# A hybrid decoder block: the first half's output projection with two of its four pairs of rows as seven-product units, and the mixers' outputs stored whole

## The chip, the cores and the metric

One core of a Trainium2 chip runs the whole layer in one launch. The metric is the device time of one execution in microseconds (us); lower is better. The engines are PE (matmuls; its weight loads are shown as PEld), DVE, ACT and POOL (elementwise work), and SP, which in this kernel issues every DMA, in the order of its own list. Each engine works through its list strictly in order.

## The reference

The layer takes x (2048 positions, 1024 columns, float32) through two mixers and an FFN:

```python
h = rmsnorm(x, norm1_g);  proj = h @ w_in
# mixer A: gated linear attention (GLA), 4 heads, chunks, a running state
o = rmsnorm(gla_chunked(q, k, v, log_a), gla_norm_g) * silu(p_g)      # 512 columns
# mixer B: gated short convolution
o_conv = c_b * causal_depthwise_conv(c_c * c_h, conv_w)               # 512 columns
x = x + concat([o_gla, o_conv]) @ w_out                               # 1024 x 1024
h2 = rmsnorm(x, norm2_g)
x = x + (silu(h2 @ w_ffn_gate) * (h2 @ w_ffn_up)) @ w_ffn_down        # 2816 wide
return rmsnorm(x, norm_f_g)
```

The line with `w_out` is the output projection that the change is about.

## The kernel before, in words

**Layout.** Everything is kept transposed: a tile has 128 columns of the model as partitions and 512 positions as elements. The 2048 positions are four blocks, two to a half; `half` and `j` count them. The 1024 columns are 8 tiles of 128. The output projection of a half therefore makes 8 rows of tiles, two blocks wide, each a sum over 8 tiles `k` of the mixers' outputs (k = 0 to 3 from GLA, 4 to 7 from the convolution).

**Float32 from pieces.** An operand is split in a high part (`split`, L162: ACT rounds it) and a low part (DVE subtracts). A product of two split tiles is three matmuls of 128x128 by 128x512: high-high, high-low, low-high. Weights are split on the way as well (`weight_quarter`, L404).

**Seven products.** Most of the kernel's products are 2x2 blocks: two rows of tiles by two blocks of positions, over operands halved in k. `unit` (L452) makes the four result blocks from seven products rather than eight, by sums and differences of the weights' quarters (A11, A12, A21, A22 and S1 to S4, `unit_weights`, L424, four POOL operations and seven splits) and of the operands (B11, B12, B21, B22 and T1 = B12 - B11, T2 = B22 - T1, T3 = B22 - B12, T4 = B21 - T2). A product is one block sum of `len(op)` slices of three matmuls (`product_step`, L443). The result blocks are put together by DVE additions (L473); with `onto` each product is added onto a given tile in SBUF as soon as it is there, and the third product goes on in the PSUM bank of the first.

**The output projection before** (`out_proj`, L935) doesn't use units: it takes the rows in four pairs (`d0` = 0, 2, 4, 6), and for each pair runs over k, with four PSUM banks, 12 matmuls for each k. In the middle of a pair it loads the residual's tiles y (from `xt`, L956); at the end DVE adds the banks to them (L970), SP stores them to `sx`, and ACT and POOL add up their squares (L921) for the next norm. Its weights come from `plain_weights` (L912): one load of 1 MB and four splits for a pair.

**The mixers' outputs before** are split where they are made and stored as pairs of high and low parts: the convolution's at L794 to L798, the GLA's at L907 to L909. `build_mix` (L929) loads pairs of 512 KB, with nothing left to do on ACT and DVE.

**What sets the order.** The body (L1250 on) runs the input projection of both halves, then `out_proj(0)`, `out_proj(1)`, then the FFN. Between matmul groups `tick` (L241) takes a step of background generators; the GLA of the second half runs so beside the first half's output projection. While the second output projection runs, `h2_first` and `h2_rest` make the FFN's first operands. A scheduler that works on the whole program then fixes each engine's list. Buffers come from pools with a fixed number of slots: 28 operand slots (`opp`, each for a high and a low part), 9 tiles `tp` (y, squares, results), 4 split weights `wqp`, 2 raw weights, 8 PSUM banks. A load into a slot stands in SP's list and waits there until the slot's last reader is done; everything behind it in the list waits too. The input unit before `out_proj(0)` fills all 28 operand slots; the plain projection needs 16.

Of the kernel before, what the change touches and what calls it, by code (L numbers as in the profile page):

```python
# [10 lines left out]
F32 = mybir.dt.float32  # L11
# [41 lines left out]
def tile_hymba_block(ctx, tc, x, xt, win, wa, wgu, wout, wffn, wdown, wdown_first, small, out):  # L53
# [57 lines left out]
    s_mix = [[dram.tile([P, 2, PB], F32, name=f"sm{b}_{k}") for k in range(4)] for b in range(NB)]  # L111
    s_gla = [dram.tile([P, HEADS, 2, PB], F32, name=f"sgla{b}") for b in range(NB)]
# [291 lines left out]
    def weight_quarter(src):  # L404

        n = src.shape[-1]
# [7 lines left out]
        split(src, h[:, 0, :], h[:, 1, :])  # L414
        return h
# [8 lines left out]
    def unit_weights(src, raw=None):  # L424
        raw = raw_weights(src) if raw is None else raw
        n = src.shape[-1]
        a11, a12, a22, a21 = [raw[:, i, :] for i in range(4)]
        s1 = rawp.tile([P, PB], F32, name="s1", tag="s1", bufs=1)[:, 0:n]
        w = {"A11": weight_quarter(a11)}
        pool.tensor_tensor(s1, a21, a22, ALU.add)  # L430
# [10 lines left out]
        return w  # L441

    def product_step(o, w, op, k, first):  # L443
# [3 lines left out]
        xh, xl = op[k][:, 0, :], op[k][:, 1, :]  # L447
# [301 lines left out]
    def in_proj(half, ops, first=None, differences=None):  # L749
# [22 lines left out]
        for i0 in (0, 2):  # L772
# [128 lines left out]
    def gla_finish(b, t, osb, g):  # L901
# [26 lines left out]

    def build_mix(half):  # L929
# [5 lines left out]
    def out_proj(half, ops, ahead=None, rest=None):  # L935
        ssq = []
        ws = chain.from_iterable(plain_weights(wout[u], 4) for u in range(4))
        for d0 in range(0, KD, 2):
            o = {(e, j): bank() for e in range(2) for j in range(2)}
            for k in range(KD):  # L940
                for e in range(2):
                    wh, wl = next(ws)
                    for j in range(2):
                        m = ops[k][j]
                        pe.matmul(o[e, j][:], wh, m[:, 0, :], start=k == 0, stop=False)  # L945
                        pe.matmul(o[e, j][:], wh, m[:, 1, :], start=False, stop=False)  # L946
                    for j in range(2):
                        pe.matmul(  # L948
                            o[e, j][:], wl, ops[k][j][:, 0, :], start=False, stop=k == KD - 1
                        )  # L950
# [318 lines left out]
    ssq = out_proj(0, build_mix(0))  # L1269
# [118 lines left out]
```

## Time and profile before

| what | value |
|---|---|
| median of 3 runs | 2060.9 us (2059.68 to 2062.77) |
| span of the profiled execution | 2059.3 us |
| busy share PE, DVE, ACT, POOL | 98%, 69%, 47%, 42% |
| first half's output projection, first matmul | at 569.6 us |
| second half's output projection, last matmuls | at 759 us |

Of the profiled execution the span is the one time that is given. Lines of a trace read: start, duration, engine, line of the kernel, operation, tile written <- tiles read, count, and in brackets the idle time ahead of it with what ended it. Group lines read: line, engine, operation, tiles, shape and count, then busy time, mean ns of one, and the idle time before. Lines of DMA issues read: tiles, queue, count, KB each, median us from issue to landing.

### The profile page before, as it was taken

The numbers are of one execution on the slowest core, as the hardware profiler recorded it, in microseconds if no ns is written. First come the engines' busy times: TensorE is split into PE (matmuls) and PEld (weight loads), VectorE is DVE, ScalarE is ACT, GpSimd is POOL, SyncE is SP. The second block draws the span as 40 slices with busy tenths as digits, with TensorE's granted clock in tenths as the row PEclk, the third lists the DMA queues.
The fourth block names the chain that finished last, engine by engine and source line by source line (L and its number), as shares of the span: only waits on it lengthen the run. The fifth ranks groups of instructions, "written<-read, shape, count | busy, mean of one in ns | idle before, by whom it ended". The sixth has DMA issues, their size and how long they took to land.

```text
span 2059.3 us, 27063 instructions
## 1 busy us (share of the span) xinstructions
PE 2018.4 (98%) x9229; PEld 1657.3 (80%) x9229; DVE 1425.3 (69%) x2128; ACT 959.7 (47%) x1918; POOL 859.8 (42%) x622
## 2 busy tenths in 40 slices
PE   7999999999999999999999999999999999999997
PEld 6877888787888888888888878787888888878786
DVE  8789686559743886676675676767666666667774
ACT  6655365765542344444444452334434444453344
POOL 0345322122102564464564345534644544435544
PEclk9999999999999999999999999999999999999998
DMA  6378485416586873545454676476444434586653
GB/s 229 116 274 278 159 319 165 143 67 194 190 296 246 311 254 130 198 181 207 156 185 143 241 264 254 185 282 257 163 164 167 175 140 169 179 309 223 234 217 126
DMA packets 188729, 421.47 MB, mean 205 GB/s; under 512 B 19792, under 2 KB 65072, under 8 KB 178992
## 3 DMA queue, kind: packets, MB, share of 16 engines
q1 hardware_dynamic: 188592, 419.76, 57.2%
q8 instruction: 72, 1.18, 0.2%
q14 instruction: 65, 0.53, 0.1%
HBM read 274.98 MB, written 144.70 MB: 204 GB/s over the span
## 4 chain that ended last, share of the span: by engine, by line
PE 84%; DVE 7%; DMA 4%; ACT 3%; issue 1%; POOL 1%; SPq 0%; DVEq 0%; ACTq 0%; POOLq 0%
PE mm L448 24%; PE mm L449 23%; PE mm L450 23%; PE mm L945 3%; PE mm L948 3%; PE mm L946 3%; DVE wq L164 2%; DVE op L164 1%; DMA op<-sa_B 1%; DMA op<-sa_T 1%; PE a_ps L702 1%; ACT wq L163 1%; DMA siT<-lo 1%; PE o_ps L869 1%; PE o_ps L871 1%
## 5 line engine op out<-in xcount | busy, mean ns | idle before, releaser
L448 PE MATMUL mm<-op,wq 128*128 128x512 f32 x2499 | 973.7, 392 | 10.3 <-ACT c L480 5.3
L449 PE MATMUL mm<-op,wq 128*128 128x512 f32 x2499 | 972.5, 390 | 1.6 <-DVE op L164 1.6
L450 PE MATMUL mm<-op,wq 128*128 128x512 f32 x2499 | 961.3, 390 | 2.6 <-DVE wq L164 2.3
L164 DVE TENSOR_TENSOR wq<-raw,wq 128x512 fp32r<-128x512 f32 (+2 forms) x626 | 508.9, 818 | 262.6 <-ACT wq L163 260.0
L163 ACT ACTIVATE wq<-raw 128x512 fp32r<-128x512 f32 (+2 forms) x626 | 364.9, 589 | 585.6 <-PE mm L450 447.9
L448 PEld LDWEIGHTS mm<-op,wq 128*128 128x128 f32 x2499 | 468.9, 188 | 114.9 <-ACT c L480 8.0
L450 PEld LDWEIGHTS mm<-op,wq 128*128 128x128 f32 x2499 | 469.1, 188 | 103.8 <-DVE wq L164 6.1
L449 PEld LDWEIGHTS mm<-op,wq 128*128 128x128 f32 x2499 | 469.3, 188 | 99.1 <-DVE op L164 3.7
L432 POOL TENSOR_TENSOR raw<-s,raw 128x512 f32<-128x512 f32 (+2 forms) x97 | 133.3, 1374 | 518.5 <-DVE wq L164 474.7
L430 POOL TENSOR_TENSOR s<-raw 128x512 f32<-128x512 f32 (+2 forms) x97 | 127.4, 1313 | 247.5 <-DMA raw<-in_wffn_dram 90.7
L473 DVE TENSOR_TENSOR c<-mm,c 128x512 f32<-128x512 f32 x198 | 135.8, 686 | 72.7 <-PE mm L450 70.9
L473 DVE TENSOR_TENSOR y<-mm,y 128x512 f32<-128x512 f32 x185 | 126.9, 687 | 83.3 <-PE mm L450 82.9
L437 POOL TENSOR_TENSOR raw<-raw 128x512 f32<-128x512 f32 (+2 forms) x97 | 120.6, 1244 | 126.7 <-DVE wq L164 126.7
L927 POOL TENSOR_TENSOR ssx<-ssx,q 128x512 f32<-128x512 f32 x52 | 77.4, 1504 | 158.8 <-ACT q L926 158.5
L431 POOL TENSOR_TENSOR raw<-raw 128x512 f32<-128x512 f32 (+2 forms) x97 | 137.3, 1416 | 4.9
L480 ACT ACTIVATE c<-mm 128x512 f32<-128x512 f32 x198 | 116.1, 587 | 11.1 <-PE mm L450 9.3
L945 PE MATMUL mm<-op,wq 128*128 128x512 f32 x256 | 100.9, 395 | 0.0
L946 PE MATMUL mm<-op,wq 128*128 128x512 f32 x256 | 99.7, 389 | 0.0
L163 ACT ACTIVATE wq<-s 128x512 fp32r<-128x512 f32 (+2 forms) x97 | 56.9, 587 | 89.3 <-PE mm L450 85.4
L164 DVE TENSOR_TENSOR wq<-s,wq 128x512 fp32r<-128x512 f32 (+2 forms) x97 | 82.6, 852 | 2.8 <-ACT wq L163 2.1
L164 DVE TENSOR_TENSOR op<-op 128x512 fp32r<-128x512 f32 x94 | 76.8, 844 | 4.7 <-ACT op L163 4.6
L948 PE MATMUL mm<-op,wq 128*128 128x512 f32 x256 | 79.8, 390 | 0.0
(204 smaller groups left out, 1807.6 us busy)
## 6 DMA issues: line engine op xcount, KB each, us to landing
raw<-in_wffn_dram SPq DMA_DIRECT2D x44, 1024.0 KB, 6.5
sa_B<-so SPq DMA_DIRECT2D x47, 512.0 KB, 4.2
op<-sa_B SPq DMA_DIRECT2D x47, 512.0 KB, 7.1
raw<-in_win_dram SPq DMA_DIRECT2D x23, 1024.0 KB, 5.4
sa_T<-so SPq DMA_DIRECT2D x44, 512.0 KB, 4.5
op<-sa_T SPq DMA_DIRECT2D x44, 512.0 KB, 6.9
raw<-in_wdown_dram SPq DMA_DIRECT2D x24, 768.0 KB, 5.8
sx<-y SPq DMA_DIRECT2D x48, 256.0 KB, 4.0
```

The lines of the kernel that those rows point to most:

```text
L163: last_hi[:] = [act.activation(hi, src, AF.Copy)]
L164: last_lo[:] = [dve.tensor_tensor(lo, src, hi.bitcast(F32), ALU.subtract)]
L430: pool.tensor_tensor(s1, a21, a22, ALU.add)
L431: pool.tensor_tensor(a21, a11, a21, ALU.subtract)
L432: pool.tensor_tensor(a11, s1, a11, ALU.subtract)
L448: pe.matmul(o[:], wh, xh, start=first and k == 0, stop=False, skip_group_check=True)
L449: pe.matmul(o[:], wh, xl, start=False, stop=False, skip_group_check=True)
L450: return pe.matmul(o[:], wl, xh, start=False, stop=k == n - 1, skip_group_check=True)
L473: dve.tensor_tensor(t[:], o[:], t[:], ALU.add)
L945: pe.matmul(o[e, j][:], wh, m[:, 0, :], start=k == 0, stop=False)
L946: pe.matmul(o[e, j][:], wh, m[:, 1, :], start=False, stop=False)
L948: pe.matmul(o[e, j][:], wl, ops[k][j][:, 0, :], start=False, stop=k == KD - 1)
```

## The change

The mixers' outputs are stored whole, as float32 (half the bytes, no split at the mixers), and split when they are loaded for the output projection, in both halves (`load_whole`).

The second half's projection is otherwise as before. In the first half's, the pairs d0 = 0 and 2 stay plain; d0 = 4 and 6 become two units of seven products, with 4 slices each (84 matmuls a unit) and `onto` the residual. `build_mix_sevens` lays the operands of both forms into the 28 slots: a slot holds the whole value in one half and the high part in the other, and for all but B21 a second slot holds the low part. While the plain pairs run, a generator `making` takes 16 steps, one for each k of the two pairs. For each of four slices POOL makes T1, T3, T2 and T4 (16 operations); T1, T2 and T3 are split over the whole values that are no longer needed. T4 is stored to DRAM and, in the second pair from its fifth k on, loaded and split over B12's high and low part (`fourth`), which only the plain pairs read.

In the units, the loads of the residual y stand at the start of each unit; each product is added onto y; the finished rows are stored and their squares added up after the unit. The weights of a unit are taken from the same 1 MB as those of a plain pair, read with a stride.

```diff
-    s_mix = [[dram.tile([P, 2, PB], F32, name=f"sm{b}_{k}") for k in range(4)] for b in range(NB)]
-    s_gla = [dram.tile([P, HEADS, 2, PB], F32, name=f"sgla{b}") for b in range(NB)]
+    s_mix = scratch("sm", 4)
+    s_gla = [dram.tile([P, HEADS, PB], F32, name=f"sgla{b}") for b in range(NB)]
+    s_mix4 = [dram.tile([P, PB], F32, name=f"smt{k}") for k in range(4)]
...
                 dve.tensor_tensor(y[:], c[:], y[:], ALU.mult)
-                hi = tp.tile([P, PB], F32R, name="hi", tag="t")
-                split(y[:], hi[:], y[:].bitcast(F32R))
-                dst = s_mix[2 * half + j][i0 + r]
-                store(dst[:, 0, :], hi[:].bitcast(F32))
-                store(dst[:, 1, :], y[:])
+                store(s_mix[2 * half + j][i0 + r][:], y[:])
...
         dve.scalar_tensor_tensor(osb[:], ot[:], col(C_GN), g[:], ALU.mult, ALU.mult)
-        split(osb[:], g[:].bitcast(F32R), osb[:].bitcast(F32R))
-        for e, y in enumerate((g, osb)):
-            store(s_gla[b][:, :, e, t * P : (t + 1) * P], y[:])
+        store(s_gla[b][:, :, t * P : (t + 1) * P], osb[:])
...
     def build_mix(half):
-        def pair(b, k):
-            return load_pair(s_gla[b][:, k] if k < HEADS else s_mix[b][k - HEADS])
-
-        return [[pair(2 * half + j, k) for j in range(2)] for k in range(KD)]
+        return [[load_whole(mixed(2 * half + j, k)) for j in range(2)] for k in range(KD)]
+
+    def build_mix_sevens():
...
+        for k in range(KD):
+            row = []
+            for j in range(2):
+                n = "B" + str(1 + k // 4) + str(1 + j)
+                o = b[n, k % 4] = slot()
+                load(whole(o), mixed(j, k))
+                lo = o[:, 1, :]
+                if n != "B21":
+                    x = t[n, k % 4] = slot()
+                    lo = x[:, 0, :]
+                split(whole(o), o[:, 0, :], lo)
...
+        def divide(y, n, m, k):
+            x = b[m, k][:, 1, :], t[m, k][:, 1, :]
+            split(y[:], *x)
+            sevens[n].append(x)
+
+        def making():
+            for k in range(4):
+                b11, b12, b22 = [whole(b[n, k]) for n in ("B11", "B12", "B22")]
+                y, z, b21 = [tt(n) for n in ("ty", "tz", "b21")]
+                load(b21[:], mixed(0, k + 4))
+                pool.tensor_tensor(y[:], b12, b11, ALU.subtract)
+                pool.tensor_tensor(z[:], b22, b12, ALU.subtract)
+                yield
+                divide(y, "T1", "B11", k)
+                divide(z, "T3", "B12", k)
+                yield
+                pool.tensor_tensor(y[:], b22, y[:], ALU.subtract)
+                yield
+                divide(y, "T2", "B22", k)
+                pool.tensor_tensor(y[:], b21[:], y[:], ALU.subtract)
+                store(s_mix4[k][:], y[:])
+                yield
+
+        def fourth(k):
+            lo, hi = t["B12", k][:, 0, :], b["B12", k][:, 0, :]
+            load(lo.bitcast(F32), s_mix4[k][:])
+            split(lo.bitcast(F32), hi, lo)
+            sevens["T4"].append((hi, lo))
...
         for d0 in range(0, KD, 2):
+            if sevens and d0 >= KD // 2:
+                onto = {}
+                for r, j in ((0, 0), (1, 1), (0, 1), (1, 0)):
+                    onto[r, j] = tt("y")
+                    load(onto[r, j][:], xt[2 * half + j, :, d0 + r, :])
+                raw = raw_weights(wout[d0 // 2]).rearrange("p a (b e c) -> p (a b) e c", e=2, c=P)
+                quads = [raw[:, 4 * h : 4 * h + 4, e, :] for e, h in ((0, 0), (0, 1), (1, 1), (1, 0))]
+                unit(None, sevens, onto=onto, raw=quads)
+                tick()
+                for r, j in ((0, 0), (1, 1), (0, 1), (1, 0)):
+                    y = onto[r, j]
+                    store(s_x1[2 * half + j][d0 + r][:], y[:])
+                    sum_squares(ssq[j], y[:], False)
+                continue
...
+                if sevens:
+                    next(ahead, None)
+                    if d0 == 2 and k >= 4:
+                        fourth(k - 4)
                 tick()
...
-    ssq = out_proj(0, build_mix(0))
+    plain, sevens, making, fourth = build_mix_sevens()
+    ssq = out_proj(0, plain, making, sevens=sevens, fourth=fourth)
```

More of the change, by code (lines that the diff above doesn't have):

```diff
@@ L413, in weight_quarter @@
             h = h[:, :, 0:n]
-        split(src, h[:, 0, :], h[:, 1, :])
+        hi, lo = h[:, 0, :], h[:, 1, :]
+        if len(src.shape) == 3:
+            hi, lo = [y.rearrange("p (k c) -> p k c", c=P) for y in (hi, lo)]
+        split(src, hi, lo)
         return h
@@ L424, in unit_weights @@
     def unit_weights(src, raw=None):
[L425 to L428, printed above, removed]
+        s1 = rawp.tile([P, PB], F32, name="s1", tag="s1", bufs=1)
+        if src is None:
+            a11, a12, a22, a21 = raw
+            s1 = s1.rearrange("p (k c) -> p k c", c=P)
+        else:
+            raw = raw_weights(src) if raw is None else raw
+            a11, a12, a22, a21 = [raw[:, i, :] for i in range(4)]
+            s1 = s1[:, 0 : src.shape[-1]]
         w = {"A11": weight_quarter(a11)}
@@ L441, in unit_weights, with parts @@
         return w
+    def parts(o):
+        return o if isinstance(o, tuple) else (o[:, 0, :], o[:, 1, :])
     def product_step(o, w, op, k, first):
@@ new lines, in build_mix_sevens, with slot, whole @@
+    def build_mix_sevens():
+        def slot():
+            return opp.tile([P, 2, PB], F32R, name="op", tag="op")
+        def whole(o):
+            return o[:, 1, :].bitcast(F32)
+        plain, sevens, b, t = [], no_operands(), {}, {}
+        for k in range(KD):
[9 more added lines that the diff above has]
+                split(whole(o), o[:, 0, :], lo)
+                row.append((o[:, 0, :], lo))
+                if n != "B12":
+                    sevens[n].append(row[-1])
+            plain.append(row)
+        def divide(y, n, m, k):
[24 more added lines that the diff above has]
+            sevens["T4"].append((hi, lo))
+        return plain, sevens, making(), fourth
@@ L936, in out_proj @@
+    def out_proj(half, ops, ahead=None, rest=None, sevens=None, fourth=None):
         ssq = []
-        ws = chain.from_iterable(plain_weights(wout[u], 4) for u in range(4))
+        ws = chain.from_iterable(plain_weights(wout[u], 4) for u in range(2 if sevens else 4))
         for d0 in range(0, KD, 2):
+            if sevens and d0 >= KD // 2:
[12 more added lines that the diff above has]
+                continue
```

17 lines of the change are left out of this document (9 added, 8 removed).

## The prediction

> **What bounds the kernel now.** I read the page from the top: the busy shares of the engines, then the shares of the chain that ended last.
>
> ```profile
> span 2059.3 us, 27063 instructions
> PE 2018.4 (98%) x9229; PEld 1657.3 (80%) x9229; DVE 1425.3 (69%) x2128; ACT 959.7 (47%) x1918; POOL 859.8 (42%) x622
> PE 84%; DVE 7%; DMA 4%; ACT 3%; issue 1%; POOL 1%; SPq 0%; DVEq 0%; ACTq 0%; POOLq 0%
> ```
>
> PE holds the span, so a matmul that goes is worth its pitch, and whatever makes PE wait costs its full length. An average doesn't tell whether PE is bound in the stage of the change, so next come the stages: the first half's output projection, which ends in the third row, and the second half's.
>
> ```profile
> 560.00:600.00 40.00, 39.51 (x216) 32.19 (x215) 22.14 (x49) 17.56 (x50) 0.00 (x0) 1.00 0.87 302
> 600.00:660.00 60.00, 60.00 (x300) 49.82 (x299) 23.95 (x45) 20.32 (x53) 14.55 (x10) 1.00 0.67 223
> 660.00:720.00 60.00, 60.00 (x263) 48.98 (x262) 42.12 (x47) 18.52 (x31) 26.57 (x18) 1.00 0.90 330
> 720.00:760.00 40.00, 40.00 (x178) 33.14 (x177) 35.14 (x36) 17.66 (x31) 28.48 (x18) 1.00 0.82 284
> ```
>
> After the window and its length come the busy times of PE, PEld, DVE, ACT and POOL, then clock, DMA share and GB/s. PE is full in all four but for 0.49 us. In the first projection DVE is busy 46 us of 100 and POOL 15: room, but not everywhere. The pitch comes from PE's first matmul there and DVE's first addition at the end of each pair of rows:
>
> ```profile
> 569.55 0.50 PE L945 MATMUL mm<-op,wq 128*128 128x512 f32 x1
> 597.54 2.47 DVE L970 TENSOR_TENSOR y<-y,mm 128x512 f32<-128x512 f32 x4
> 623.40 2.65 DVE L970 TENSOR_TENSOR y<-y,mm 128x512 f32<-128x512 f32 x4 [3.34 <-PE mm L948]
> 647.98 2.65 DVE L970 TENSOR_TENSOR y<-y,mm 128x512 f32<-128x512 f32 x4 [2.55 <-PE mm L948]
> 669.74 2.65 DVE L970 TENSOR_TENSOR y<-y,mm 128x512 f32<-128x512 f32 x4 [2.49 <-PE mm L948]
> ```
>
> The last pair holds nothing but its 96 matmuls: 669.74 - 647.98 = 21.76 us, 0.2267 us each. The first took 28.0 us, so that 6.2 us of it went to the small matmuls of the attention (GLA) that runs beside it; the second holds 4.1 us of them, the third 2.8.
>
> **The change, part by part.** *Fewer matmuls.* Two pairs of rows were 192 matmuls. Two units of seven products, each of 4 slices and 3 matmuls, are 168. The built instruction lists agree. 24 x 0.2267 = **-5.4 us**. This is all there is to gain on PE.
>
> *Splits that move.* The 32 splits of the mixers' outputs leave the input projections; 32 come back after the loads, 16 in each output projection.
>
> ```profile
> L164 DVE TENSOR_TENSOR c<-c,hi 128x512 fp32r<-128x512 f32 x4 | 2.7, 684 | 0.0
> L163 ACT ACTIVATE op<-h 128x512 fp32r<-128x512 f32 x16 | 9.5, 625 | 10.0 <-PE mm L948 9.1 <-DVE h L615 0.9
> L164 DVE TENSOR_TENSOR op<-h,op 128x512 fp32r<-128x512 f32 x16 | 16.3, 1051 | 3.0 <-ACT op L163 3.0
> PE sc L845 <- DVE kq L835: 1.3, 1, 1.3
> ```
>
> A split is 0.63 us on ACT and 0.68 on DVE, 1.05 where POOL runs beside it. What leaves is off the path: the one wait of PE on DVE's attention work there is 1.3 us, so the relief is worth 0 to 1.3, and I take 0, because that wait stands ahead of the second half's first split. In the second projection 16 more splits are 11 to 17 us of DVE beside the 77 of 100 in the rows above. They stand ahead of the heavy work on the next operands; 0 to 2 us, taken 0.
>
> *More beside the first projection.* DVE gets 16 splits of loads, 12 of differences, 4 of the fourth operand, 6 of weights (14 for 8) and 6 additions (14 for 8): 44, at 0.68 to 1.05 us 30 to 46 us on top of the 46, within the 95 that remain of the stage's 100.2. POOL gets 16 differences and 8 weight operations. On average this is hidden; what matters is who stands behind whom. These are the prices:
>
> ```profile
> L927 POOL TENSOR_TENSOR ssx<-ssx,q 128x512 f32<-128x512 f32 x28 | 42.9, 1556 | 109.1 <-ACT q L926 109.1
> L430 POOL TENSOR_TENSOR s<-raw 128x512 f32<-128x512 f32 x2 | 2.6, 1296 | 7.8 <-DMA raw<-in_wffn_dram 7.8
> y<-in_xt_dram SPq DMA_DIRECT2D x32, 256.0 KB, 5.2
> sx<-y SPq DMA_DIRECT2D x32, 256.0 KB, 3.5
> raw<-in_wout_dram SPq DMA_DIRECT2D x7, 1024.0 KB, 7.5
> op<-sfT SPq DMA_DIRECT2D x4, 256.0 KB, 2.8
> 597.72 2.35 SPq L145 DMA_DIRECT2D kq<-sk  x4
> ```
>
> A POOL operation is 1.3 us alone and 1.56 in company; a 256 KB load lands 2.8 to 5.2 us after its issue, a store 3.5; SP spends 0.59 us on each of the small GLA loads. Nothing in the trace of before shows this mixture, so each place is bounded.
>
> (a) *The last input unit.* ACT's list now has the split of the first loaded operand ahead of the copy that frees a bank for the unit's third product. That operand's slot comes free with the unit's third matmul, and its load follows 1 MB of weights. Landing 2.8 to 7.5 us later against some 10 us of PE work ahead of that product: a wait of 0 to 1.5, taken 0.4.
>
> (b) *The first plain pair.* The operands now fill all 28 slots, and k = 4 to 7 are loaded behind 14 GLA loads (8.2 us of SP), these behind the mixer's last store, some 3 us into the stage. So k = 4 can be issued at 11 us, lands 2.8 later and is split 1.3 after that: at 15 us, where PE wants it after 48 matmuls and some 3.4 us of GLA, at 14.3. Behind k = 4 differences that wait for POOL stand among the splits. In the built list PE has been given 12 matmuls of the next pair to do here. 0 to 3 us, taken 0.8.
>
> (c) *The first unit.* Before, the residual y was loaded in the middle of a pair and needed at its end. A unit adds each product onto y at once, and its third product writes to the bank that DVE must have added up first. In SP's list y stands behind the four stores of the pair just ended, and these behind the last fourth operand's store and its load, on whose landing SP itself must wait. Count from the end Z of the plain pairs: four additions 2.65, stores' issues 0.6, the load, 2.8 to 5.2, and the addition, 0.68: Z + 6.7 to 9.1. PE wants it after 24 matmuls and eight small GLA ones, which took 1.9 us here:
>
> ```profile
> 588.00 0.38 PE L869 MATMUL o_ps<-vt,scores 128*128 128x128 f32 x2
> ...
> 589.88 0.66 PE L876 MATMUL kv<-vt,ee 128*64 128x128 f32 x8
> ```
>
> That is Z + 7.3, with Z at 54 us after the start (192 matmuls and the 10.3 above). But DVE's four additions stand behind the split of the third fourth operand. Its difference is the ninth POOL operation after the first pair's end (31.5 us: 113 matmuls, since PE's list mixes the pairs, and 5.8 of small ones), so it is made at 44 to 47; stored, loaded and split 7.6 to 10 later. Then y is issued at Z + 3.2 to 6, and at the late end PE waits 4.6. 0 to 4.6, taken **2.2**.
>
> (d) *The second unit.* It is worse placed. Let T be the end of the first unit's last product. DVE's list reads: split of the second projection's first operand, addition of that last product, further splits. SP's list: load of that operand, three more, the store of the finished row, and only then the second unit's y. So the load (issued near T - 2.5, landed at T + 0.3 to 2.7), its split (1.3), the addition (0.7), two issues on SP (0.8), y's load (2.8 to 5.2) and its addition (0.7) follow each other: T + 6.6 to 11.4. PE has 22 matmuls to do, until T + 5.0. A wait of 1.6 to 6.4; I take **3.4**, below the middle, since late landings would hardly come twice. What is queued behind that addition on DVE are the splits of the unit's last weights, which only wait with PE.
>
> Here the Trainium skill speaks against me. "DMA: Bandwidth & Descriptors", Anatomy of one DMA, gives about 2.0 us and a transfer at 436 GB/s, for DMAs issued from GpSimd: 2.6 us for 256 KB by an estimate. By it (c) would be nothing and (d) about 1.2, and the sum 3 us under before. The rows above, 5.2 for these very loads with the queues this full, decide against it.
>
> Sum: -5.4 + 0.4 + 0.8 + 2.2 + 3.4 = **+1.4 us**, 2060.7 against the profiled execution's span of 2059.3, the one time shown of it; that is 1.6 under the median of the runs, 2060.9, so the forecast is **2062 us**.
>
> **The rivals.**
>
> *The saving comes through.* If the loads land in 2.8 us and POOL runs at 1.3, (a) to (c) vanish and (d) is 1.6: 2060.9 - 5.4 + 1.6 = 2057.1, and with the full relief of 1.3 in the input projections 2055.8; I give it 2056. For it: PE's built list has other work at the tight spots, and DMA traffic falls, as 16 pair loads of 512 KB become 256. Against it: (d) has no such work, and its loads go out together.
>
> *The residual's loads hold up both units, and the clock falls with them* (slower). This trace shows what a pause does. Near the start PE did nothing from 11.3 to 16.4 us but four short transposes:
>
> ```profile
> 7.29 4.04 PE L599 MATMUL xt<-ident,xr 128*128 128x128 f32 x24 [0.28 <-DMA xr<-in_x_dram]
> 13.32 0.64 PE L555 MATMUL rb_ps<-ident,rep 128*128 128x128 f32 x4 [1.98 <-DVE rep L552]
> 16.39 0.73 PE L362 MATMUL mm<-op,wq 128*128 128x512 f32 x1 [2.42 <-ACT op L163]
> ...
> 19.90 0.39 PE L362 MATMUL mm<-op,wq 128*128 128x512 f32 x1
> ```
>
> ```profile
> 15.00:18.00 3.00, 1.61 (x4) 1.33 (x5) 2.90 (x5) 1.93 (x4) 0.00 (x0) 0.75 1.02 402
> 18.00:21.00 3.00, 3.00 (x10) 2.34 (x10) 2.96 (x6) 3.00 (x7) 0.00 (x0) 0.68 1.06 389
> PE mm L448 <- ACT c L480: 5.3, 4, 1.7
> ```
>
> Behind it the granted clock was 0.75 and 0.68, and the 8 matmuls from 16.39 to 19.90 took 3.5 us instead of 1.8: 1.7 lost. With (c) at 4.6 and (d) at 6.4, such a dip after (d) alone and (a) and (b) as taken, the sum is -5.4 + 1.2 + 11.0 + 1.7 = +8.5: 2069.4. It decides from the point where waits and dip together pass 9.5. For it: both chains run through SP's one list, with 5.2 us a load. Against: of PE's waits on the unit products, the row last quoted, the longest was 1.7 us.
>
> That a pause brings the slow clock is also the rule in the Trainium skill's "TensorE: Matmul & The Clock Gate", What's actually happening: an idle window of about 3.4 us halves the clock until a busy one has passed. The dip above fits it.
>
> *DVE falls behind in the plain pairs.* In (b) splits and differences come one upon the other while POOL subtracts; at 1.05 us and more for each of the 11 or 12 between k = 4 and k = 6, DVE needs 12 us for what PE does in 7 to 8, less what the pulled-up matmuls cover. A wait of 4 to 5 in place of 0.8, the rest as taken: 2066. Against: DVE's average there.
>
> **How the numbers follow.** A measurement of this kernel can tell some 0.2%, 4.1 us, from no change. The forecast, waits that eat the saving (2057 to 2065), has 0.50; the saving that comes through, 0.17; the loads with the clock, 0.22; DVE behind, 0.11. Hence faster 0.17, same 0.50, slower 0.33. The forecast's own range is 2057 to 2065. The bounds together reach from 2055.8 (above) to 2060.9 - 5.4 + 1.5 + 3 + 4.6 + 6.4 + 2 + 1.7 = 2074.7; the range for 8 in 10 leaves out the far end: 2056 to 2071.
>
> **What would show it.** In the profile after: 168 unit matmuls after 192 plain ones; no PE wait over 0.5 us in the plain pairs (else b or DVE); in each unit one wait ahead of the third product, on DVE's addition into y, of 0 to 4.6 and of 1.6 to 6.4 us, with the y load the last to land before it; clock 1.00 throughout, unless a wait passes 3 us. The forecast is wrong if neither unit shows a wait (then under 2057), or if PE idles in the plain pairs or in the second projection for more than 4 us.

## The result, and the profile after

The changed kernel takes 2076.0 us (median of 6 runs, 2074.2 to 2078.8) beside 2060.9 of the kernel before on the same chip: 1.0068 times as long, 95% interval 1.0057 to 1.0079. The forecast was 2062, the range 2056 to 2071. It is slower by 15 us where I had expected no difference.

The first rows of the page, the kernel after:

```profile
span 2077.1 us, 27053 instructions
PE 2022.9 (97%) x9205; PEld 1658.1 (80%) x9205; DVE 1449.0 (70%) x2156; ACT 969.6 (47%) x1940; POOL 892.0 (43%) x646
PE 79%; DVE 8%; DMA 5%; ACT 3%; issue 3%; POOL 1%; SPq 1%; DVEq 0%; ACTq 0%; POOLq 0%
```

PE has its 24 matmuls less and is yet busy 4.5 us longer, since matmuls under a slow clock count as busy. The chain that ended last runs 79% over PE instead of 84. The four windows of the prediction, for the kernel after (window, length, PE, PEld, DVE, ACT, POOL, clock, DMA share, GB/s):

```profile
560.00:600.00 40.00, 36.70 (x192) 28.22 (x191) 30.82 (x55) 21.39 (x57) 11.32 (x9) 0.97 0.78 241
600.00:660.00 60.00, 56.32 (x274) 45.50 (x273) 46.40 (x69) 28.96 (x69) 30.93 (x22) 0.96 0.56 186
660.00:720.00 60.00, 56.42 (x234) 45.44 (x233) 40.63 (x60) 27.60 (x48) 18.50 (x12) 0.94 0.69 237
720.00:760.00 40.00, 40.00 (x178) 33.11 (x178) 37.64 (x35) 11.84 (x21) 30.41 (x20) 1.00 0.89 290
```

PE idles in three of the four and the clock is 0.94 to 0.97 there. DVE is busy 77 us in the first two instead of 46, much of it with operations that take longer. Four landmarks divide the run; these are single instructions from the timeline, of the kernel after:

```profile
573.92 0.50 PE L1022 MATMUL mm<-op,wq 128*128 128x512 f32 x1
612.35 0.69 DVE L1050 TENSOR_TENSOR y<-y,mm 128x512 f32<-128x512 f32 x1 [2.47 <-PE mm L1026]
639.62 2.47 DVE L1050 TENSOR_TENSOR y<-y,mm 128x512 f32<-128x512 f32 x4
776.71 0.39 PE L459 MATMUL mm<-op,wq 128*128 128x512 f32 x1
```

and the one of before that the prediction doesn't show, the FFN's first matmul:

```profile
759.87 0.39 PE L448 MATMUL mm<-op,wq 128*128 128x512 f32 x1
```

| stretch (profiled executions) | before | after | difference |
|---|---|---|---|
| up to the first plain matmul | 569.6 | 573.9 | +4.4 |
| the two plain pairs, up to the first addition of the second | 53.9 | 65.7 | +11.8 |
| from there to the FFN's first matmul | 136.5 | 137.1 | +0.6 |
| the rest of the span | 1299.4 | 1300.4 | +1.0 |

The third stretch should have been shorter by the 5.4 of the 24 matmuls, so that 6.0 us are lost in it too. Two thirds of the 17.8 us between the two spans stand in the plain pairs, where I had put 0.8. PE's waits in the projections, the kernel after, 560 to 700 us (total, times, longest):

```profile
PE mm L459 <- DVE y L484: 4.2, 2, 3.6
PE v_ps L861 <- ACT wq L164: 2.4, 1, 2.4
PE mm L1023 <- DVE op L165: 2.0, 2, 1.5
PE kt_ps L858 <- DVE kvs L893: 0.7, 1, 0.7
PE mm L1022 <- DMA op<-sm: 0.6, 1, 0.6
PE mm L1022 <- ACT op L164: 0.6, 1, 0.6
```

The first row is the units (0.6 and 3.6), the others, 6.3 us, are the plain pairs and the recurrence beside them: 10.5 us in all, 0.5 before. The prediction had named PE idle for more than 4 us in the plain pairs as a sign of being wrong. Behind the waits the clock falls (windows again; the clock is the third number from the end):

```profile
595.00:605.00 10.00, 7.99 (x25) 5.23 (x24) 10.00 (x18) 6.44 (x20) 4.98 (x4) 0.66 0.66 212
674.00:680.00 6.00, 5.66 (x14) 4.45 (x15) 2.22 (x5) 2.02 (x4) 1.29 (x1) 0.52 1.00 336
```

It is 0.66 in the first plain pair and 0.52 behind the wait of 3.6 us: twelve matmuls from 674.34 to 679.63 took 5.3 us instead of 2.7. By the clock of the first three of the four windows above, the slow clock cost some 7 us (an estimate: each length times what its clock lacks of 1.00). With the waits that is nearly all the loss of these stretches, 11.8 and 6.0.

Ahead of the stage, of the 4.4, these two are in the rows of 285 to 300 us, where before has none:

```profile
PE ot L912 <- DVE osb L905: 1.6, 1, 1.6
PE mm L459 <- DVE c L484: 0.6, 1, 0.6
```

They come back, to 0.1 us, in all of e1 to e11 below, which store the first half's outputs whole only. No stored output is loaded yet at that time (the first such load is issued at 545.6 us), and DVE is busy 13.75 us of the 14 from 285 to 299, before 13.62: its list has another order there. Why wasn't taken apart. Of the other 2.2 us most is a slow clock at 163 us (0.66 from 163 to 168), which this execution has, the slowest of the six, and those of e2 to e5 haven't; these begin 1.1 to 2.3 us later than before.

### The profile page after: what moved, and what is told of

It is laid out like the page before. It is cut to its first block, busy times and chain, and to the rows that moved or that the text cites. A ratio compares the mean times of both kernels' runs of the same rounds, so it can differ in the third digit from the quotient of the medians.

```text
span 2077.1 us, 27053 instructions
## 1 busy us (share of the span) xinstructions
PE 2022.9 (97%) x9205; PEld 1658.1 (80%) x9205; DVE 1449.0 (70%) x2156; ACT 969.6 (47%) x1940; POOL 892.0 (43%) x646
## 4 chain that ended last, share of the span: by engine, by line
PE 79%; DVE 8%; DMA 5%; ACT 3%; issue 3%; POOL 1%; SPq 1%; DVEq 0%; ACTq 0%; POOLq 0%
PE mm L459 24%; PE mm L460 24%; PE mm L461 24%; DVE op L165 2%; DVE wq L165 1%; PE mm L1023 1%; PE mm L1026 1%; PE mm L1022 1%; DMA op<-shT 1%; PE a_ps L713 1%; SPq L146 1%; ACT wq L164 1%; ACT op L164 1%; DMA op<-sgla 1%; DMA siT<-lo 1%
## 5 line engine op out<-in xcount | busy, mean ns | idle before, releaser
L459 PE MATMUL mm<-op,wq 128*128 128x512 f32 x2555 | 996.9, 393 | 16.4 <-ACT c L491 7.0
L460 PE MATMUL mm<-op,wq 128*128 128x512 f32 x2555 | 996.0, 390 | 0.4 <-DVE op L165 0.2
L461 PE MATMUL mm<-op,wq 128*128 128x512 f32 x2555 | 984.4, 391 | 2.7 <-DVE wq L165 2.7
L459 PEld LDWEIGHTS mm<-op,wq 128*128 128x128 f32 x2555 | 480.6, 188 | 123.4 <-ACT c L491 8.8
L461 PEld LDWEIGHTS mm<-op,wq 128*128 128x128 f32 x2555 | 480.6, 188 | 107.0 <-DVE wq L165 6.5
L460 PEld LDWEIGHTS mm<-op,wq 128*128 128x128 f32 x2555 | 480.8, 188 | 100.5 <-DVE op L165 2.5
L438 POOL TENSOR_TENSOR s<-raw 128x512 f32<-128x512 f32 (+2 forms) x99 | 132.5, 1338 | 270.0 <-DMA raw<-in_wffn_dram 88.2
L484 DVE TENSOR_TENSOR y<-mm,y 128x512 f32<-128x512 f32 x199 | 136.2, 686 | 91.8 <-PE mm L461 88.9
L165 DVE TENSOR_TENSOR op<-op 128x512 fp32r<-128x512 f32 x130 | 108.4, 860 | 20.7 <-ACT op L164 20.5
L164 ACT ACTIVATE op<-op 128x512 fp32r<-128x512 f32 x130 | 76.5, 622 | 26.4 <-DMA op<-sgla 13.0
L1023 PE MATMUL mm<-op,wq 128*128 128x512 f32 x192 | 76.2, 398 | 2.1 <-DVE op L165 2.0
L1022 PE MATMUL mm<-op,wq 128*128 128x512 f32 x192 | 75.2, 398 | 1.2 <-DMA op<-sm 0.6
```

Source lines behind the costliest of these rows:

```text
L164: last_hi[:] = [act.activation(hi, src, AF.Copy)]
L165: last_lo[:] = [dve.tensor_tensor(lo, src, hi.bitcast(F32), ALU.subtract)]
L459: pe.matmul(o[:], wh, xh, start=first and k == 0, stop=False, skip_group_check=True)
L460: pe.matmul(o[:], wh, xl, start=False, stop=False, skip_group_check=True)
L461: return pe.matmul(o[:], wl, xh, start=False, stop=k == n - 1, skip_group_check=True)
L484: dve.tensor_tensor(t[:], o[:], t[:], ALU.add)
```

## The experiments

Three theories stood first, each able to carry the whole loss. **A**: POOL's subtractions slow DVE's splits, and PE starves. **B**: the loads of the plain operands come late. **C**: the splits moved behind the loads unsettle other stages. The table gives medians, each against before's median measured together with it, and the stretches of the profiled execution as above (first plain matmul; plain pairs; from there to the FFN).

| kernel | us | over before | ratio, 95% interval | first | pairs | to FFN |
|---|---|---|---|---|---|---|
| before | 2060.9 | | | 569.6 | 53.9 | 136.5 |
| the change | 2076.0 | +15.1 | 1.0068, 1.0057 to 1.0079 | 573.9 | 65.7 | 137.1 |
| e1 whole, plain | 2068.3 | +7.6 | 1.0039, 1.0026 to 1.0052 | 577.7 | 53.0 | 136.5 |
| e2 differences late | 2087.8 | +27.1 | 1.0130, 1.0115 to 1.0145 | 571.9 | 62.3 | 149.6 |
| e3 differences on DVE | 2070.6 | +9.9 | 1.0044, 1.0027 to 1.0061 | 571.7 | 59.6 | 137.4 |
| e4 no differences | 2069.5 | +8.8 | 1.0044, 1.0028 to 1.0061 | 570.6 | 56.7 | 139.1 |
| e5 y early | 2074.3 | +11.8 | 1.0050, 1.0032 to 1.0068 | 570.8 | 63.8 | 135.3 |
| e6 y early, DVE | 2066.1 | +3.6 | 1.0018, 1.0009 to 1.0027 | 573.0 | 57.5 | 136.5 |
| e7 second half in parts | 2084.6 | +23.0 | 1.0109, 1.0093 to 1.0125 | 571.3 | 67.2 | 143.2 |
| e8 all three | 2065.7 | +4.1 | 1.0023, 1.0014 to 1.0033 | 572.1 | 59.4 | 130.1 |
| e9 units, 16 slots | 2066.2 | +4.7 | 1.0025, 1.0016 to 1.0035 | 578.3 | 53.0 | 132.6 |
| e10 e8, differences shifted | 2072.8 | +11.4 | 1.0052, 1.0036 to 1.0067 | 571.5 | 58.6 | 137.5 |
| e11 first half whole, plain | 2067.6 | +6.2 | 1.0028, 1.0019 to 1.0038 | 575.0 | 53.0 | 136.5 |
| e12 parts and whole | 2081.1 | +18.9 | 1.0086, 1.0069 to 1.0103 | 582.3 | 65.3 | 131.4 |
| e13 e12, differences shifted | 2076.0 | +13.8 | 1.0065, 1.0050 to 1.0080 | 580.9 | 61.4 | 132.0 |

### e1: stored whole, four plain pairs

```diff
-    plain, sevens, making, fourth = build_mix_sevens()
-    ssq = out_proj(0, plain, making, sevens=sevens, fourth=fourth)
+    ssq = out_proj(0, build_mix(0))
```

> One part of the change alone: the mixers' outputs are stored whole and split after the load, and all four pairs of rows of the first half stay plain (no differences, no units). Theory A (the subtractions on GpSimd slow VectorE's splits, and TensorE starves in the plain pairs): this part costs little; the first plain pair takes 28 to 30 us from its first matmul to its first addition (28.0 before, 38.4 after the change), and the total is 2061 to 2065. Theory B (the loads of the first pair's operands land late, behind the recurrence's loads in SP's list): the first pair still takes 33 us or more, total 2066 to 2071. Theory C (the splits moved out of the input projections unsettle these): the first plain matmul starts 4 us later than before whatever follows.

Half of the loss is here, and not where I looked: the plain pairs take 53.0, less than before. It is all ahead of them: the 2.2 us of 291 to 297, and in the last unit of the input projections

```profile
569.24 0.79 PE L459 MATMUL mm<-op,wq 128*128 128x512 f32 x1 [3.40 <-DVE c L484]
```

On DVE that addition stood behind six splits of loaded operands, here the last four:

```profile
566.02 0.68 DVE L165 TENSOR_TENSOR op<-op 128x512 fp32r<-128x512 f32 x1
566.70 1.88 DVE L165 TENSOR_TENSOR op<-op 128x512 fp32r<-128x512 f32 x3
568.51 1.28 DVE L484 TENSOR_TENSOR c<-mm,c 128x512 f32<-128x512 f32 x2
```

DVE was busy without a break from 550 to 570 us and waited for no load, so PE waited for the splits' own time. The clock fell behind it (0.57 from 569 to 576 us). C holds: the first plain matmul comes 8.1 us late.

### e2, e3, e4: when, where and whether the differences are made

e2 begins them at the second pair, two steps per k; e3 makes them on DVE; e4 leaves them out.

```diff
-                    next(ahead, None)
+                    for _ in range(d0):
+                        next(ahead, None)
```

> The changed kernel with its differences begun only at the second plain pair, two steps of the generator per k in place of one, so that nothing of them lies beside the first pair. Theory A: the first pair falls from 38.4 to 28 to 31 us, the second rises from 27.3 to 32 to 38, total 2068 to 2080. Theory B: the first pair stays at 34 us or more, total 2078 or more.

```diff
-                pool.tensor_tensor(y[:], b12, b11, ALU.subtract)
+                dve.tensor_tensor(y[:], b12, b11, ALU.subtract)
...
```

> The changed kernel with the sixteen subtractions of the differences on VectorE in place of GpSimd. Theory A: the splits beside them go back from 1.1 to 1.8 us to about 0.7, VectorE gets 16 x 0.7 = 11 us of more work but saves more than that; the first pair takes 30 to 34 us, the total is 2066 to 2072. If it is not GpSimd but simply too much work on VectorE, or theory B, the first pair stays at 37 us or more and the total at 2074 or more.

```diff
-    plain, sevens, making, fourth = build_mix_sevens()
-    ssq = out_proj(0, plain, making, sevens=sevens, fourth=fourth)
+    plain, sevens, _, _ = build_mix_sevens()
+    sevens.update(T1=sevens["B11"], T3=sevens["B22"], T2=sevens["B22"], T4=sevens["B21"])
+    ssq = out_proj(0, plain, iter(()), sevens=sevens, fourth=lambda k: None)
```

> The changed kernel without any differences: the two units take B11, B22, B22 and B21 in the place of T1 to T4, so the first half's output projection is not the reference's, and 16 subtractions, 16 splits and the fourth operand's trip through DRAM are left out. Theory A: the first pair takes 28 to 30 us, no wait of TensorE over 0.5 us in the plain pairs or in the recurrence beside them, total 2062 to 2067 (what is left are the residual's waits in the units). Theory B: first pair 34 us or more, total 2072 or more.

e3 gives 5.1 us back, as A has it (first pair 34.0). The groups of DVE's splits by shape, 570 to 640 us (count, busy, mean ns of one, idle before), the change first:

```profile
L165 DVE TENSOR_TENSOR op<-op 128x512 fp32r<-128x512 f32 x15 | 15.0, 1010 | 7.7 <-ACT op L164 7.7
L165 DVE TENSOR_TENSOR wq<-raw,wq 128x512 fp32r<-128x512 f32 x8 | 8.0, 1002 | 0.4 <-ACT wq L164 0.3
L165 DVE TENSOR_TENSOR op<-ty,op 128x512 fp32r<-128x512 f32 x7 | 7.8, 1113 | 0.2 <-ACT op L164 0.2
L165 DVE TENSOR_TENSOR op<-tz,op 128x512 fp32r<-128x512 f32 x4 | 4.6, 1140 | 0.1
```

and e3:

```profile
L165 DVE TENSOR_TENSOR op<-op 128x512 fp32r<-128x512 f32 x15 | 11.9, 801 | 6.5 <-ACT op L164 6.5
L165 DVE TENSOR_TENSOR op<-ty,op 128x512 fp32r<-128x512 f32 x7 | 5.4, 781 | 0.0
```

The same 15 and 7 splits take 0.80 and 0.78 us instead of 1.01 and 1.11, though DVE now makes the differences too. The Trainium skill says why in "GPSIMD Engine Reference", 1. Specifications: GpSimd's way into SBUF is VectorE's as well, and VectorE's instructions with two inputs from SBUF contend with it; a split has two such inputs. The rows agree.

The times of the first pair can't be set against the 28.0 of before, as my forecasts did, since PE's list mixes the pairs differently in each kernel: by the first addition PE had begun 96 plain matmuls before the change, 107 in the change, 110 in e3, 112 in e2 and e4. PE's waits in that pair and the clock tell more: 3.2 us at a clock of 0.91 in the change; at a clock of 1.00, 0.7 in e3, 1.2 in e2 and 2.2 in e4. So A isn't all: with no differences at all 2.2 us of waits stay in e4 (first pair 35.3, total between the two forecasts). But e2 doesn't speak against A, though its first pair (34.3) and its total carry B's numbers: with the differences gone from the first pair, the waits there fall by 2 us and the slow clock is gone. Its total comes from 7.3 and 7.7 us of waits in the units, onto which the late work was pushed.

### e9: the slots

The plain operands come from `build_mix(0)`, 16 slots; the units take the same tiles, and the residuals are loaded early as in e5.

```diff
-    plain, sevens, making, fourth = build_mix_sevens()
-    ssq = out_proj(0, plain, making, sevens=sevens, fourth=fourth)
+    plain = build_mix(0)
...
+    B.update(T1=B["B11"], T3=B["B22"], T2=B["B22"], T4=B["B21"])
+    ssq = out_proj(0, plain, iter(()), sevens=B, fourth=lambda k: None)
```

> Units of seven products on the sixteen operands of the plain pairs alone: T1 to T4 are B11, B22, B22 and B21 again, so the first half's output projection is not the reference's, and the twelve further operand slots, the differences and their splits are left out; the residuals are loaded ahead of the first unit. Theory S (the first pair starves because its operands' loads wait for slots: all 28 are taken, in the changed kernel the last eight loads are issued from 585.7 to 599.2 us, before the change from 552 to 573): the first pair has no wait over 0.5 us, as in the kernel with four plain pairs, and from the first plain matmul to the 744th takes 184 to 187 us (202.8 in the changed kernel, 184.9 for as many matmuls before). If the loads are late for another reason (the recurrence's loads in SP's list), the first pair keeps waits of 2 us or more and the stretch takes 190 us or more. The total also holds what the last unit of the input projections loses to earlier splits (3.4 us and a slow clock in the kernel with four plain pairs): 2062 to 2068.

The issues of the last eight operands' loads on SP (start, us, count): before (first and last row of four), the change, and e9:

```profile
552.36 2.01 SPq L145 DMA_DIRECT2D op<-sm  x3
...
571.27 1.50 SPq L145 DMA_DIRECT2D op<-sm  x3
```

```profile
585.67 0.90 SPq L146 DMA_DIRECT2D op<-sm  x2
588.99 0.90 SPq L146 DMA_DIRECT2D op<-sm  x2
592.31 1.56 SPq L146 DMA_DIRECT2D op<-sm  x2
599.15 0.93 SPq L146 DMA_DIRECT2D op<-sm  x2
```

```profile
554.71 2.37 SPq L146 DMA_DIRECT2D op<-sm  x4
559.36 3.07 SPq L146 DMA_DIRECT2D op<-sm  x4
```

With 16 slots the plain pairs take 53.0 us and PE doesn't wait in them (e1, with the residual in its old place, has the same); with 28, 56.7 (e4). So B holds, by the slots: with 16 the loads stand ahead of the recurrence's in SP's list, with 28, of which the later ones come free only with the last input unit, behind them, as step (b) had read off the list. By then no slot is waited for: from 565 to 600 us none of SP's waits in e4 is on a matmul of the last input unit, so it is the order of the list that costs. And in the change the last two stand behind more: SP waited with the store of the first T4, which stands ahead of them (585 to 600 us):

```profile
SPq L149 <- POOL ty L985: 4.4, 1, 4.4
```

This store is issued at 598.32, those loads at 599.15. The two projections together take 185.6 us in e9 and 190.3 before: 4.7 less, with one wait of 1.0: the saving of the 24 matmuls is real. Theory S came as forecast, stretch and total. But the early loads bring e1's wait back (3.5 us on DVE's addition at 569.89, and the clock), so that the total is still 4.7 over before. Like e4, e9 leaves out the differences, so it shows where time goes and is no version of the layer.

### e5, e6: the residual's place

Both units' residuals are loaded ahead of the first unit; for that, the squares of this half use another pool's buffers. e6 also has the subtractions on DVE.

```diff
-                    onto[r, j] = tt("y")
-                    load(onto[r, j][:], xt[2 * half + j, :, d0 + r, :])
+                for u in (4, 6) if d0 == 4 else ():
...
+                        load(y[:], xt[2 * half + j, :, u + r, :])
```

> The changed kernel with the residual of both units loaded ahead of the first unit (the squares of this half use buffers of another pool, so that eight residual tiles can be held at once); the differences stay on GpSimd. If the waits of the two units (0.6 and 3.6 us, and the slow clock of about 2.5 us behind the second) come from the residual's place in SP's list, as steps (c) and (d) of the prediction have it, both are under 0.5 us and the total falls by 5 to 7 from the changed kernel's 2076, to 2069 to 2071. If VectorE is simply late there (its additions stand behind splits of the second projection's operands), the second unit's wait stays at 3 us or more and the total at 2074 or more.

> Both repairs at once: the subtractions on VectorE and the residuals ahead of the first unit. If GpSimd's subtractions (5.4 us, the difference of the medians with them on GpSimd and on VectorE) and the residual's place (waits of 2.7 and 3.8 us in that kernel, and about 3 us of slow clock behind them) are two separate causes, the total is 2070.6 less 6 to 9: 2061 to 2065, within 0.2% of before, and what is left over the saving of 5.4 is the 2 us lost in the input projections and the first pair. If VectorE's load is the common cause, the units' waits stay over 3 us in sum and the total is 2068 or more.

In the change SP's list reads as step (d) had it (start, us, count):

```profile
663.09 4.39 SPq L146 DMA_DIRECT2D op<-sgla  x4
668.28 0.32 SPq L149 DMA_DIRECT2D sx<-y  x1
668.66 1.94 SPq L146 DMA_DIRECT2D y<-in_xt_dram  x4
```

The load's landing released DVE's addition at 673.60, and that PE at 674.34. With the load ahead, this wait is gone in both kernels. e5's loss is 3.3 less than the change's, e6's 6.3 less than e3's. Neither total is where the first forecast had it: e5's is the rival's, without the rival's wait, and e6's lies between the two. In both another wait takes the place of the old one, 1.7 us in e5, and here in e6, on ACT and then on PE:

```profile
663.11 0.63 ACT L164 ACTIVATE op<-op 128x512 fp32r<-128x512 f32 x1 [10.43 <-DMA op<-sgla]
...
666.51 0.61 ACT L164 ACTIVATE wq<-raw 128x512 fp32r<-128x512 f32 x1
```

```profile
667.18 0.80 PE L459 MATMUL mm<-op,wq 128*128 128x512 f32 x1 [4.35 <-ACT wq L164]
```

ACT waits 10.4 us for the second projection's first operand, to split it, and 1.2 for another; the unit's weight splits stand behind. These are the splits that I had moved at no cost.

### e7, e8: the second half in parts again

The second half's outputs are split at the mixers and stored as pairs, as before the change; e8 has all three repairs.

```diff
+                if not half:
+                    store(dst[:], y[:])
+                    continue
+                hi = tp.tile([P, PB], F32R, name="hi", tag="t")
+                split(y[:], hi[:], y[:].bitcast(F32R))
```

> The changed kernel, but the second half's mixers' outputs are stored in two parts as before the change (split where they are made, loaded as 512 KB pairs), so that no split of the second projection's operands stands on ScalarE and VectorE beside the units. If those splits, which wait for their loads, hold up the units' weight splits and additions (ScalarE waited 10.4 us for such a load ahead of a weight split in the kernel with both repairs), the second unit's wait of 3.6 us and its slow clock of 2.5 shrink: total 2068 to 2073. If the residual's own place in SP's list is the cause, the wait stays and the total is 2074 to 2077, since the second half's splits go back to the mixers at no cost there (they were there before).

> The three repairs at once: subtractions on VectorE, the residuals ahead of the first unit, and the second half's mixers' outputs in two parts. The last wait of the units in the kernel with the first two (4.35 us behind a weight split on ScalarE, and some 2.5 us of slow clock) should go: 2066.1 less 5 to 7, 2059 to 2062 with before at 2061 to 2062.5: the same or up to 0.15% faster. If the wait goes over to a load of a pair of 512 KB in place of a split, the total stays at 2065 or more.

e8 does what was meant: no wait over 0.3 us is left in the units, and the last stretch takes 130.1, 6.4 less than before. The total stays, at the rival's number but without its wait on a pair's load: 2.5 ahead, 5.5 in the plain pairs, and 2.9 in the FFN's first unit, in two waits that before doesn't have (760 to 790 us):

```profile
PE mm L459 <- ACT c L491: 1.8, 1, 1.8
PE mm L459 <- ACT wq L164: 1.1, 1, 1.1
```

e7 alone went against both forecasts: it loses 7.9 us more than the change. There SP had eight loads of pairs, 512 KB each, ahead of the residual (663.19 to 668.50), and DVE's addition waited for it:

```profile
678.64 2.01 DVE L484 TENSOR_TENSOR y<-mm,y 128x512 f32<-128x512 f32 x3 [6.32 <-DMA y<-in_xt_dram]
```

PE lost 8.5 us to that instead of 3.6. Four times the bytes ahead of the residual (8 x 512 KB for 4 x 256) more than doubled the wait, which bears out its place in the list as the cause of (d). And the recurrence's splits, back beside the plain pairs and POOL's subtractions, came with waits of 3.8 and 2.8 us there, 0.7 and 2.4 in the change.

### e10: differences shifted

```diff
-                    next(ahead, None)
+                    for _ in range((k >= 4) if d0 == 0 else 1 + (k < 4)):
+                        next(ahead, None)
```

> The kernel with all three repairs, and the differences begun at the second half of the first pair (four steps there, twelve in the second pair). If the differences' splits beside the first half of the first pair add to its lateness, the first pair's waits (2.0 us) and slow clock (about 2 us) shrink and the total is 2062 to 2064; if that lateness is the slots' alone, nothing changes there, and the later differences press on the units: 2065 to 2070.

The pairs gain 0.8 us; a wait of 3.3 us on a weight split appears at 739.6, in the second projection. The total is above both forecasts.

### e11: only the first half stored whole

Four plain pairs (e1) with e7's storing of the second half.

> Four plain pairs as before, only the first half's mixers' outputs stored whole, the second half's in two parts as before. If the losses of the kernel with all outputs stored whole (2.2 us at 291 to 297 us, and 3.4 us with a slow clock at 569 us; 7.6 in the medians) come from the first half's splits after the load, both stay here and the total is 2066 to 2069. If they come from the second half's outputs, the total is 2061 to 2063.

Both waits stay (2.2 and 3.35 us): it is the first half's outputs. This execution had no slow clock behind the 3.35.

### e12, e13: parts for the plain pairs, whole for the differences

The mixers' outputs are stored in parts, the first half's also whole; the 16 plain operands take the first slots and need no split; T1 to T3 lie in the other 12, into which the whole values are loaded. e13 adds e10's edit.

```diff
+                if not half:
+                    store(s_mixw[j][i0 + r][:], y[:])
+                    lo = tp.tile([P, PB], F32R, name="lo", tag="t")[:]
...
+        plain = build_mix(0)
...
+                x = t[n, k] = slot()
+                load(x[:, 1, :].bitcast(F32), whole_mixed(j, d))
```

> Every mixer's output stored in two parts as before, so that no loaded operand of the plain pairs has to be split, and the first half's also whole, for the differences alone; the sixteen plain operands take the first slots, T1 to T3 the twelve behind them; subtractions on VectorE, residuals ahead of the first unit. If the losses ahead of the output projection (2.2 us at 291 to 297 us, 3.4 us at 569) and in its first pair come from the split after the load and from the order of the slots, all of them go and the saving of 24 matmuls comes through: 2055 to 2060. If they go over to the added transfers (16 stores and 12 loads of 256 KB) the total is 2062 or more, with waits on loads in the plain pairs.

> The same with the differences begun at the second half of the first pair. If VectorE's subtractions wait for the twelve added loads in the first pair and hold up what stands behind them, this one is faster than its sister by 1 to 4 us; if not, the two agree within 1 us or this one is slower for pressing on the units.

The rival came true. What was aimed at went: the waits at 291 to 297 and 569 are gone, the first pair takes its operands without a wait (28.2 us to its first addition in e12), and the units are clean (131.4 and 132.0). But the first plain matmul is 12.8 and 11.4 us late, and a wait stands in the plain pairs. PE's longest waits in e12, 200 to 700 us:

```profile
PE mm L1034 <- ACT wq L166: 7.1, 1, 7.1
PE mm L461 <- DVE c L486: 4.1, 2, 3.9
PE mm L461 <- ACT c L493: 3.1, 1, 3.1
```

The first is in the plain pairs, at 620 us: ACT's split of the second pair's weights waited for their load, which SP issued only at 613.27. The other two are ahead of the stage, 3.9 at 402 and 3.1 at 287 us, and new; e13 has them too (3.7 and 3.1). e13 is 5.1 us faster than e12, more than the 1 to 4 forecast. What in the added stores, tiles and loads makes these waits wasn't taken apart. No version ran that beats the kernel before; nearest are e6 and e8, 3.6 and 4.1 us over.

## Why the prediction was wrong

**24 matmuls, -5.4.** Right: e9's two projections are 4.7 shorter, with a wait of 1.0 in them. e8's last stretch is 6.4 shorter by DVE's additions, 4.9 from the end of the two plain pairs on PE.

**Splits that move, 0.** This step failed first; e1, which has it alone, costs 7.6. I counted DVE's and ACT's time over a stage, and there the time was; what I didn't price is what stands behind a split in its list. Where slots are free (e1, e9, e11), six splits in a row hold up an addition in the last input unit, by their own time, and PE waits 3.4 to 3.5 us. In the second unit a split waits 10.4 us for its load on ACT, the unit's weight splits wait behind it, and PE loses 4.35 (e6). The 2.2 us at 291 to 297 come with the first half's outputs stored whole; there my 0 to 1.3 of relief was a loss, and its cause stays open.

**(a), 0.4.** The place was right, the way it happens not. In the change it costs nothing, as the 28 slots delay the loads. Where they come early PE waits 3.4, past my bound of 1.5, and not on ACT's copy behind a landing load but on DVE's addition behind six splits.

**(b), 0.8.** The step that failed most: the plain pairs lost 11.8, and my bound was 3. I had the late loads and their place in SP's list, and the first of them was issued 11.8 us into the stage, where I had put 11. But I counted no more than the first: the last went out at 25.2, behind the difference's store. And I had DVE keep up beside POOL's subtractions. To price the two, the table's stretch isn't good enough, since it ends at a DVE addition that may come late itself. On PE the same 192 plain and 102 small matmuls stand ahead of the first unit's first matmul, here in e9, e4, e3 and the change:

```profile
633.05 0.47 PE L459 MATMUL mm<-op,wq 128*128 128x512 f32 x1
629.06 0.47 PE L459 MATMUL mm<-op,wq 128*128 128x512 f32 x1
629.38 0.48 PE L459 MATMUL mm<-op,wq 128*128 128x512 f32 x1
640.14 0.47 PE L459 MATMUL mm<-op,wq 128*128 128x512 f32 x1
```

From the first plain matmul that is 54.7, 58.4, 57.7 and 66.2 us, in one execution each: slots and late loads 3.7, differences made on DVE nothing that shows, POOL's subtractions 8.5. They make DVE's splits slower, and the store ahead of the last two loads later (598.32, in e3 594.98). In the medians the subtractions on POOL cost 8.2 where the residual is loaded early (e5 less e6) and 5.1 where it isn't (the change less e3, whose units wait 2.3 us longer). The slower DVE was my rival "DVE falls behind", at 0.11, with 4 to 5 us at its place; splits at 1.0 to 1.14 us were in it, the recurrence's waits of 0.7 and 2.4 and the clock were not.

**(c), 2.2.** Measured 0.6, within its bounds of 0 to 4.6.

**(d), 3.4.** Measured 3.6, with the load, the split, the addition and y in the order given. What I left to a rival was the clock behind it: 2.6 us.

**The rivals.** I priced the slow clock after (d) alone and DVE's delay alone. They came together, with the moved splits on top.

**The other price of a load.** The estimate of 2.6 us for 256 KB, from the Trainium skill's "DMA: Bandwidth & Descriptors", Anatomy of one DMA, would have made (d) 1.2. The four loads issued from 668.66 landed late enough for 3.6.

## What to carry to other kernels

Work moved from a producer to behind a load is not the same work: look up in each in-order list what stands behind it, and price that at the load's wait, or at the time of all the moved operations that stand there in a row, and not at the engine's average. Before filling the last slots of a pool, look up when the stage before gives them back and what then stands ahead of their loads in the queue. And beside a VectorE that the bottleneck waits for, make the differences on VectorE itself rather than on GpSimd: on GpSimd the same 16 subtractions cost 5 to 8 us here.

## What the runs showed of the hardware

Matmuls run at 0.43 us instead of 0.23 behind pauses of PE of 3.40 (e1), 3.58 (the change) and 4.35 us (e6), for 12 to 14 matmuls; but not behind one of 3.35 (e11), whose first rows after it are

```profile
569.25 0.50 PE L459 MATMUL mm<-op,wq 128*128 128x512 f32 x1 [3.35 <-DVE c L484]
569.59 0.39 PE L460 MATMUL mm<-op,wq 128*128 128x512 f32 x1
```

and in e5 they did behind a pause of 1.68 us, beginning 1.6 us after its end. The length of a pause alone doesn't tell: at 163 us the change has a pause of 2.07 us and then the clock of 0.66, e13 in the same place one of 2.08 and a clock of 1.00. And in the first plain pair the clock fell to 0.66 around four waits of 0.6 to 1.5 us, where the prediction had expected it only behind a wait over 3.

The Trainium skill's "TensorE: Matmul & The Clock Gate", What's actually happening, has a window of 3413 ns that runs freely, and the slow clock after an idle one. A pause of 3.58 or 4.35 us can hold such a window; 3.35 and 3.40 both lie just under it, and only behind the second was the clock slow. The dips behind 1.68 and 2.07 us it doesn't explain, nor, as the prediction took it to, the one near the start, where the two pauses are 1.98 and 2.42 us with 0.64 us of transposes between them.
